# Block products of an MLP's down projection, spread over both up chunks of a pair and summed over the layer

## The chip, the cores and the metric

The kernel runs on 1 core of one Trainium2 chip. The metric is device microseconds of one execution. Before the change it is 2117.61 us, the median of 3 runs (2116.02 to 2118.4). The profile shows one further execution, which took 2115.5 us; its span in the trace is 2113.7 us.

## The reference, cut to what matters

```python
D_MODEL = 2048; SEQ = 256; DEPTH = 2; D_FF = 4 * D_MODEL      # float32

def _mlp(h, w_up, w_down):
    return jnp.square(jax.nn.relu(h @ w_up)) @ w_down

for layer in range(DEPTH):
    ...                                        # attention and pooling (even), gated convolution (odd)
    x = x + _mlp(_rmsnorm(x, mlp_norm_g[layer]), w_mlp_up[layer], w_mlp_down[layer])
```

The change is in `_mlp`, which runs once in each of the two layers: 256 tokens, an up matrix of 2048 x 8192 and a down matrix of 8192 x 2048, 64 MB each. The weights are read from HBM once.

## The kernel before, in words

**Numbers.** TensorE works on float32r, a shortened float32. Every weight and every activation is therefore split into `hi` (its rounded value) and `lo` (the rest). A weight slab of 1 MB (512 rows by 512 columns, tile `raw`, two buffers) arrives by a DMA of SyncE's queue. ScalarE casts half a slab to `hi` (L140), VectorE subtracts to get `lo` (L141), and a ring of six `hi` and six `lo` buffers holds what TensorE is to read next. Three products (hi·hi, hi·lo, lo·hi) make one full product.

**The MLP in chunks.** The 8192 hidden columns are 16 up chunks of 512, taken as 8 pairs. `up_chunk(c)` multiplies the normalised, turned input `xT` with 4 slabs (64 couples of a 128x512 matmul, L160, and a 128x256 matmul, L161), then makes the hidden tile `hT` in two halves: a copy on ScalarE (`t`, L194), a sum on VectorE (`h`, L196), ReLU and square on ScalarE (L728, L730), and a split into hi and lo (L200, L201). The next user of the chunk needs `hT`.

**The down projection.** For the first seven pairs, columns 0 to 1023 of the output are made by `down_seven`: a 2x2 block scheme with seven products instead of eight, on sums and differences of blocks of the weights (`b`, three buffers, 128x2048 each) and of the activations (`fT`, four forms made by `sum_forms` on VectorE and ScalarE). Each product is 12 matmuls (L764 to L766). I call them p1, p5, the one of `form(3)`, p6 (`form(2)`), p7 (`form(0)`), and the two last ones, which read `hT` alone. Columns 1024 to 2047 are made by `down_block(pair, 2)` and `down_block(pair, 3)`, plain blocks of 48 matmuls each (L153 to L155). The eighth pair is made of four plain blocks.

**Sums into x.** The result of a product or a plain block goes from PSUM into the residual `x` with the token's scale `r2`: one VectorE instruction of 128x512 each (`onto`, L790; L850 for the plain blocks). Within a pair, `down_seven` keeps products in SBUF tiles `part` (copied by ScalarE, L779), combines them with 4 additions (L783) and does 7 `onto`: 11 VectorE instructions of 128x512 a pair.

**The order.** Each engine runs its own instructions in a fixed order. The kernel's code is written as generators, and a scheduler orders the instructions of each engine from the order of the calls. Per pair the calls before were: five products, with one slab of the first up chunk (2p+2; I call it chunk A) behind each of the first four; the rest of chunk A; the two last products; the whole second up chunk (2p+3, chunk B); two plain blocks. PSUM has 4 buffers of two banks: chunk A or B takes two, and products (two to a buffer) and plain blocks take the others.

## Time and profile before

| what | us |
|---|---|
| the profiled execution, whole | 2115.5 |
| its span in the trace | 2113.7 |
| TensorE matmuls, busy | 2047.5 |
| VectorE, busy | 1535.1 |
| ScalarE, busy | 1126.1 |
| stretch of the first layer's MLP that holds its pairs | about 327 to 1014 |
| stretch of the second layer's MLP | about 1428 to 2114 |

The page of a profile lists the busy time of each engine, then groups of instructions with the mean time of one and the idle time of the engine just before them, with what ended it. Three more views of the same trace are used below: the waits (who waited for whom, total, times, longest), windows (busy time of each engine and the granted TensorE clock in a stretch), and the timeline (instructions one by one, with start, duration, and in brackets the idle time ahead of them). Matmuls overlap in the timeline, so what one costs is the distance between two starts and not its duration. Times within the trace are counted from the start of the span.

### The profile page before, as it was taken

The numbers are of one execution on the slowest core, as the hardware profiler recorded it, in microseconds if no ns is written. First come the engines' busy times: TensorE is split into PE (matmuls) and PEld (weight loads), VectorE is DVE, ScalarE is ACT, GpSimd is POOL, SyncE is SP. The second block draws the span as 40 slices with busy tenths as digits, with TensorE's granted clock in tenths as the row PEclk, the third lists the DMA queues.
The fourth block names the chain that finished last, engine by engine and source line by source line (L and its number), as shares of the span: only waits on it lengthen the run. The fifth ranks groups of instructions, "written<-read, shape, count | busy, mean of one in ns | idle before, by whom it ended". The sixth has DMA issues, their size and how long they took to land.

```text
span 2113.7 us, 26545 instructions
## 1 busy us (share of the span) xinstructions
PE 2047.5 (97%) x10534; PEld 1745.7 (83%) x10534; DVE 1535.1 (73%) x1843; ACT 1126.1 (53%) x1500; POOL 52.5 (2%) x76
## 2 busy tenths in 40 slices
PE   8999999999999999999999999999999999999999
PEld 8987888778787887888788888887878787787887
DVE  5667659787787877776566656569778787887864
ACT  5466556555555545555444444456555555555552
POOL 1340000000000000000000000000000000000000
PEclk9999999999999999999999999999999999999999
DMA  7554466555656555545555555465565655556544
GB/s 241 167 180 147 142 200 196 179 179 166 211 164 203 173 179 179 173 151 194 199 183 193 182 186 193 159 220 169 190 199 161 212 179 182 176 167 202 168 165 161
DMA packets 195820, 384.20 MB, mean 182 GB/s; under 512 B 6224, under 2 KB 16336, under 8 KB 195696
## 3 DMA queue, kind: packets, MB, share of 16 engines
q1 hardware_dynamic: 195312, 382.23, 55.7%
q8 instruction: 82, 1.34, 0.3%
q0 software_dynamic: 352, 0.27, 0.1%
q14 instruction: 42, 0.34, 0.0%
q10 hardware_dynamic: 32, 0.01, 0.0%
HBM read 380.39 MB, written 2.10 MB: 181 GB/s over the span
## 4 chain that ended last, share of the span: by engine, by line
PE 88%; DVE 6%; ACT 3%; issue 1%; POOL 1%; DMA 1%; SPq 0%; ACTq 0%; DVEq 0%; POOLq 0%
PE ps L160 31%; PE ps L161 16%; PE ps L153 10%; PE ps L155 10%; PE ps L154 10%; PE ps L764 3%; PE ps L766 3%; PE ps L765 3%; DVE lo L141 1%; DVE x L790 1%; DVE part L783 1%; ACT hi L140 1%; DVE hT L201 1%; ACT sq L730 1%; ACT h L728 1%
## 5 line engine op out<-in xcount | busy, mean ns | idle before, releaser
L160 PE MATMUL ps<-xT,hi 128*128 128x512 f32 x2816 | 1016.6, 402 | 3.8 <-ACT hi L140 3.2
L141 DVE TENSOR_TENSOR lo<-raw,hi 128x1024 fp32r<-128x1024 f32 (+2 forms) x610 | 735.9, 1225 | 334.6 <-ACT hi L140 333.1
L140 ACT CAST hi<-raw 128x1024 fp32r<-128x1024 f32 (+2 forms) x610 | 629.3, 1048 | 506.6 <-PE ps L160 141.8
L161 PE MATMUL ps<-xT,lo 128*128 128x256 f32 x2816 | 802.6, 286 | 43.7 <-DVE lo L141 43.5
L160 PEld LDWEIGHTS ps<-xT,hi 128*128 128x128 f32 x2816 | 540.7, 192 | 134.6 <-PE ps L766 5.4
L161 PEld LDWEIGHTS ps<-xT,lo 128*128 128x128 f32 x2816 | 542.0, 192 | 53.7 <-DVE lo L141 49.5
L153 PE MATMUL ps<-hi,hT 128*128 128x512 f32 (+1 forms) x896 | 349.2, 390 | 0.0
L155 PE MATMUL ps<-hi,hT 128*128 128x512 f32 (+1 forms) x896 | 347.5, 388 | 0.0
L154 PE MATMUL ps<-lo,hT 128*128 128x512 f32 (+1 forms) x896 | 347.0, 387 | 0.0
L140 ACT CAST hi<-b 128x1024 fp32r<-128x1024 f32 x196 | 206.0, 1053 | 219.1 <-PE ps L160 118.8
L141 DVE TENSOR_TENSOR lo<-b,hi 128x1024 fp32r<-128x1024 f32 x196 | 238.5, 1220 | 76.2 <-ACT hi L140 76.1
L153 PEld LDWEIGHTS ps<-hi,hT 128*128 128x128 f32 x896 | 168.3, 188 | 35.1 <-issue 1.3
L155 PEld LDWEIGHTS ps<-hi,hT 128*128 128x128 f32 x896 | 168.2, 188 | 34.9
L154 PEld LDWEIGHTS ps<-lo,hT 128*128 128x128 f32 x896 | 168.3, 188 | 33.4
L194 ACT COPY t<-ps 128x512 f32<-128x512 f32 x88 | 50.8, 580 | 70.9 <-PE ps L161 70.9
L764 PE MATMUL ps<-hi,fT 128*128 128x512 f32 x224 | 88.4, 394 | 0.0
L766 PE MATMUL ps<-hi,fT 128*128 128x512 f32 x224 | 87.7, 392 | 0.0
L765 PE MATMUL ps<-lo,fT 128*128 128x512 f32 x224 | 87.1, 389 | 0.0
L196 DVE TENSOR_TENSOR h<-ps,t 128x512 f32<-128x512 f32 x64 | 43.7, 686 | 34.1 <-ACT t L194 34.1
L764 PE MATMUL ps<-hi,hT 128*128 128x512 f32 x168 | 65.8, 393 | 0.2 <-ACT hT L200 0.2
L786 DVE TENSOR_TENSOR b<-b,b 128x2048 f32<-128x2048 f32 x28 | 64.0, 2287 | 2.7 <-DMA b<-in_w_mlp_down 2.2
L765 PE MATMUL ps<-lo,hT 128*128 128x512 f32 x168 | 65.5, 390 | 0.0
(184 smaller groups left out, 1635.7 us busy)
## 6 DMA issues: line engine op xcount, KB each, us to landing
raw<-in_w_mlp_up SPq DMA_DIRECT2D x128, 1024.0 KB, 5.3
raw<-in_w_mlp_down SPq DMA_DIRECT2D x72, 1024.0 KB, 5.2
b<-in_w_mlp_down SPq DMA_DIRECT2D x56, 1024.0 KB, 6.0
raw<-in_odd_w_in SPq DMA_DIRECT2D x48, 1024.0 KB, 5.2
raw<-in_even_w_out SPq DMA_DIRECT2D x16, 1024.0 KB, 5.2
raw<-in_odd_w_out SPq DMA_DIRECT2D x16, 1024.0 KB, 5.3
raw<-in_even_w_in SPq DMA_DIRECT2D x8, 1024.0 KB, 5.6
raw<-in_even_w_in SPq DMA_DIRECT2D x7, 1088.0 KB, 6.6
```

Source lines behind the costliest of these rows:

```text
L140: a = nc.scalar.copy(h, r)
L141: v = nc.vector.tensor_tensor(out=l, in0=r, in1=h.bitcast(F32), op=ALU.subtract)
L153: nc.tensor.matmul(o, lhsT=a_hi, rhs=hi[:, c0:c0 + n], start=first, stop=False)
L154: nc.tensor.matmul(o, lhsT=a_hi, rhs=lo[:, c0:c0 + n], start=False, stop=False)
L155: nc.tensor.matmul(o, lhsT=a_lo, rhs=hi[:, c0:c0 + n], start=False, stop=last)
L160: nc.tensor.matmul(o, lhsT=hi[:, c0:c0 + P], rhs=act[:, kt, :], start=first, stop=False)
L161: nc.tensor.matmul(o[:, S:2 * S], lhsT=lo[:, c0:c0 + P], rhs=act[:, kt, 0:S], start=False, stop=last)
L194: nc.scalar.copy(t, ps[:, :, S:2 * S])
L764: nc.tensor.matmul(o, lhsT=a_hi, rhs=hi, start=q == 0, stop=False)
L765: nc.tensor.matmul(o, lhsT=a_hi, rhs=lo, start=False, stop=False)
L766: nc.tensor.matmul(o, lhsT=a_lo, rhs=hi, start=False, stop=q == 3)
L786: nc.vector.tensor_tensor(out=out_, in0=a, in1=b, op=ALU.subtract)
```

## The change

It does three things in `mlp`, and one beside it.

1. **Order.** `up_chunk` and `down_block` yield more often, and the loop over the pairs calls them so: five products between the four slabs of chunk A as before; then the first half of plain block 2, the end of chunk A (its `hT`), the second half of plain block 2; then the sixth product, a slab of chunk B, the seventh product, the other slabs of chunk B; the first half of plain block 3, the end of chunk B, the second half of plain block 3. So one plain block now stands behind each up chunk, where both stood behind chunk B.
2. **Sums.** p1, p5, p6 and p7 are no longer combined and scaled in each pair. They are added into four SBUF tiles `totals` over the layer (`summed`: ScalarE copies in the first pair, VectorE additions from PSUM in the next six). At the seventh pair four `onto` and four additions bring them into `x`. A pair does 3 `onto` as before for the other three products. The count over a layer falls from 77 to 53 VectorE instructions of 128x512, and from 14 to 4 ScalarE copies.
3. **`hT` by halves.** `up_chunk` yields after each half, so that the scheduler sees the halves apart.
4. **Tiles.** Two small tiles move to pools that are freed earlier, and `R` gets one buffer, which makes room for `totals`. No instruction changes there.

```diff
+            hid[c] = hT
+            if seven:
+                sums[c] = fT
             for i, ps in enumerate(pss):
                 u = sum_halves(ps, "h")
...
                     sum_forms(fT[:, i], sq.rearrange("p e (t s) -> p (e t) s", t=T))
-            hid[c] = hT
-            if seven:
-                sums[c] = fT
+                yield
...
-            def kept(o):
-                part = pools["forms"].tile([P, NB], F32, tag="part", name=uid("part"), bufs=3)
-                nc.scalar.copy(part, o)
-                return part
+            def summed(name, o):
+                if pair == 0:
+                    totals[name] = pools["forms"].tile([P, NB], F32, tag=name, name=uid(name), bufs=1)
+                    nc.scalar.copy(totals[name], o)
+                else:
+                    plus(totals[name], totals[name], o)
...
-            s1 = kept(one[:, 0, :])
+            summed("p1", one[:, 0, :])
...
-            s5 = kept(one[:, 1, :])
-            onto(0, 0, s1)
+            summed("p5", one[:, 1, :])
...
-            plus(s1, two[:, 1, :], s1)
+            summed("p6", two[:, 1, :])
...
-            e = pools["forms"].tile([P, NB], F32, tag="part", name=uid("part"), bufs=3)
-            plus(e, three[:, 0, :], s1)
-            onto(1, 0, e)
-            plus(s1, s1, s5)
-            onto(0, 1, s1)
-            plus(s5, e, s5)
-            onto(1, 1, s5)
+            summed("p7", three[:, 0, :])
...
+            if pair == pairs - 2:
+                onto(0, 0, totals["p1"])
+                plus(totals["p6"], totals["p6"], totals["p1"])
+                plus(totals["p7"], totals["p7"], totals["p6"])
+                onto(1, 0, totals["p7"])
+                plus(totals["p6"], totals["p6"], totals["p5"])
+                onto(0, 1, totals["p6"])
+                plus(totals["p7"], totals["p7"], totals["p5"])
+                onto(1, 1, totals["p7"])
...
                     if i == 0:
                         flush()
+                        yield
...
         for p in range(pairs - 1):
-            products, slabs = down_seven(p), up_chunk(2 * p + 2)
+            products = down_seven(p)
+            slabs, block = up_chunk(2 * p + 2), down_block(p, 2, False)
             next(products)
-            for at in range(5):
+            for at in range(4):
                 next(products)
-                if at < 4:
-                    next(slabs)
-            whole(slabs)
-            whole(products)
-            whole(up_chunk(2 * p + 3))
-            for b in (2, 3):
-                down_block(p, b, False)
+                next(slabs)
+            next(products)
+            for steps in (block, slabs, slabs, block, slabs):
+                next(steps, None)
+            slabs, block = up_chunk(2 * p + 3), down_block(p, 3, False)
+            for steps in (products, slabs, products, slabs, slabs, slabs, block, slabs, slabs, block, slabs):
+                next(steps, None)
```

**Place 1, the end of chunk A (second pair of the first layer).** On TensorE before, the two last products follow p7, and chunk B follows them; these are the last rows of the seventh product (`ps_4209`) and the first of chunk B (`ps_4231`, `ps_4232`):

```order
L764 MATMUL ps_4209<-hi_4214,hT_3683 128x512
L765 MATMUL ps_4209<-lo_4215,hT_3683 128x512
L766 MATMUL ps_4209<-hi_4214,hT_3683 128x512
L160 MATMUL ps_4231<-xT_2333,hi_4235 128x512
L160 MATMUL ps_4232<-xT_2333,hi_4235 128x512
L161 MATMUL ps_4231<-xT_2333,lo_4236 128x256
```

From the end of chunk A to that first `L160` stand 36 matmuls: p7 and the two last products, 12 each. With the change, on TensorE too, p7 (`ps_4117`) is followed by the plain block (`ps_4139`):

```order
L765 MATMUL ps_4117<-hi_4122,fT_3785 128x512
L766 MATMUL ps_4117<-lo_4123,fT_3785 128x512
L767 MATMUL ps_4117<-hi_4122,fT_3785 128x512
L153 MATMUL ps_4139<-hi_4142,hT_3465 128x512
L154 MATMUL ps_4139<-lo_4143,hT_3465 128x512
L155 MATMUL ps_4139<-hi_4142,hT_3465 128x512
```

Behind its 48 matmuls come the 12 of the sixth product and then chunk B, whose first slab has the halves 4269 (lo 4270) and 4273: 72 matmuls instead of 36 stand between the two chunks. The seventh product has moved behind the first slab of chunk B.

On VectorE at the same place before, the sums of the products stand between the steps that make `hT` and `fT`; `lo_4236`, which chunk B waits for, comes four rows behind the last row shown here:

```order
L783 TENSOR_TENSOR part_4146<-ps_4125,part_3880 128x512
L745 TENSOR_TENSOR f_4164<-sq_4160,f_4164 128x128
L790 SCALAR_TENSOR_TENSOR x<-part_4146,r_2931,x 128x512
L783 TENSOR_TENSOR part_3880<-part_3880,part_3949 128x512
L201 TENSOR_TENSOR hT_4153<-sq_4160,hT_4153 128x2x256
L790 SCALAR_TENSOR_TENSOR x<-part_3880,r_2931,x 128x512
L783 TENSOR_TENSOR part_3949<-part_4146,part_3949 128x512
L746 TENSOR_TENSOR f_4164<-sq_4160,f_4164 128x128
L790 SCALAR_TENSOR_TENSOR x<-part_3949,r_2931,x 128x512
L196 TENSOR_TENSOR h_4172<-ps_3883,t_4170 128x512
L201 TENSOR_TENSOR fT_4154<-f_4164,fT_4154 128x512
L790 SCALAR_TENSOR_TENSOR x<-ps_4125,r_2931,x 128x512
```

With the change one addition, that of p7, is left there (`p_3428`; the first half's `h_4178`, a `lo` and an `f` stand ahead of these rows, and the last row is chunk B's first half slab):

```order
L787 TENSOR_TENSOR p_3428<-p_3428,ps_4117 128x512
L746 TENSOR_TENSOR f_4185<-sq_4181,f_4185 128x128
L196 TENSOR_TENSOR h_4193<-ps_3877,t_4191 128x512
L201 TENSOR_TENSOR hT_4174<-sq_4181,hT_4174 128x2x256
L747 TENSOR_TENSOR f_4185<-sq_4181,f_4185 128x128
L141 TENSOR_TENSOR lo_4245<-b_4242,hi_4244 128x1024
L201 TENSOR_TENSOR fT_4175<-f_4185,fT_4175 128x512
L745 TENSOR_TENSOR f_4200<-sq_4196 128x256
L141 TENSOR_TENSOR lo_4249<-b_4242,hi_4248 128x1024
L201 TENSOR_TENSOR hT_4174<-sq_4196,hT_4174 128x2x256
L746 TENSOR_TENSOR f_4200<-sq_4196,f_4200 128x128
L141 TENSOR_TENSOR lo_4270<-raw_4267,hi_4269 128x1024
```

What moved: of the eight sums that stood among these steps (three additions, five `onto`, one of them the row behind those shown) one addition is left at the place, and the two `lo` of the sixth product are new in it.

**Place 2, the end of chunk B.** With the change, one plain block (48 matmuls) stands on TensorE between the end of chunk B and p1 of the next pair, whose last three matmuls read the second half of chunk B's `hT`; before, both plain blocks stood there. These are VectorE's rows from chunk B's `h_4497` to the second half of its `hT_4493`, with the change:

```order
L196 TENSOR_TENSOR h_4497<-ps_4265,t_4495 128x512
L141 TENSOR_TENSOR lo_4569<-b_4561,hi_4568 128x1024
L790 TENSOR_TENSOR b_4561<-b_4629,b_4561 128x2048
L201 TENSOR_TENSOR hT_4493<-sq_4500,hT_4493 128x2x256
L745 TENSOR_TENSOR f_4504<-sq_4500 128x256
L196 TENSOR_TENSOR h_4512<-ps_4266,t_4510 128x512
L746 TENSOR_TENSOR f_4504<-sq_4500,f_4504 128x128
L141 TENSOR_TENSOR lo_4590<-raw_4587,hi_4589 128x1024
L747 TENSOR_TENSOR f_4504<-sq_4500,f_4504 128x128
L141 TENSOR_TENSOR lo_4594<-raw_4587,hi_4593 128x1024
L201 TENSOR_TENSOR fT_4494<-f_4504,fT_4494 128x512
L201 TENSOR_TENSOR hT_4493<-sq_4515,hT_4493 128x2x256
```

The subtraction of two weight blocks (`b_4561`, 128x2048) for the next pair's p5 now stands ahead of `hT`; before it stood behind both halves.

**Place 3, SyncE's queue at the end of chunk A.** With the change the slabs of the plain block (`raw_4140`, `raw_4206`) stand among blocks `b`, whose transfers wait until VectorE has read the buffer that they reuse:

```order
L128 DMA raw_4075<-in_w_mlp_up 128x4x512
L128 DMA raw_4140<-in_w_mlp_down 128x4x512
L758 DMA b_4242<-in_w_mlp_down 128x4x512
L128 DMA raw_4206<-in_w_mlp_down 128x4x512
L758 DMA b_4561<-in_w_mlp_down 128x4x512
L128 DMA raw_4267<-in_w_mlp_up 128x4x512
```

Before, the sixth product's block stood at the same place and chunk B's slabs behind it. What moved is that a slab of a plain block now waits behind `b_4242`, and chunk B's first slab behind `b_4561`, a block of the next pair.

## The prediction

> **What bounds the kernel now.** I read the page first, then the waits of TensorE, then windows and timelines around one wait.

> ```profile
> span 2113.7 us, 26545 instructions
> PE 2047.5 (97%) x10534; PEld 1745.7 (83%) x10534; DVE 1535.1 (73%) x1843; ACT 1126.1 (53%) x1500; POOL 52.5 (2%) x76
> L161 PE MATMUL ps<-xT,lo 128*128 128x256 f32 x2816 | 802.6, 286 | 43.7 <-DVE lo L141 43.5
> ```

> TensorE is busy 97% of the span and VectorE 73%, so the sum of VectorE's work binds nothing; it can only be late somewhere. The third row says where: the second matmul of a chunk's couple, which needs `lo`. The waits of TensorE over the whole span, and then those between 940 and 1050 us alone, give the number of times:

> ```profile
> PE ps L161 <- DVE lo L141: 43.5, 13, 3.6
> ...
> PE ps L160 <- ACT hi L140: 3.2, 1, 3.2
> PE ps L161 <- DVE lo L141: 0.2, 1, 0.2
> ```

> One of the 13 is 0.2 us, at the end of the first layer's MLP; the other 12 share 43.3 us, 3.6 each. Going through the span stretch by stretch I find one at the end of chunk A in pairs one to six of each layer, and none in the seventh, whose chunks need no forms. Here is one, on TensorE's timeline (p7 begins at 545.37; the fourth row holds two couples' first matmuls):

> ```profile
> 545.37 0.39 PE L764 MATMUL ps<-hi,fT 128*128 128x512 f32 x1
> ...
> 553.36 0.39 PE L766 MATMUL ps<-hi,hT 128*128 128x512 f32 x1
> 553.59 0.91 PE L160 MATMUL ps<-xT,hi 128*128 128x512 f32 x2
> 558.12 0.58 PE L161 MATMUL ps<-xT,lo 128*128 128x256 f32 x1 [3.62 <-DVE lo L141]
> ...
> 560.63 0.63 PE L160 MATMUL ps<-xT,hi 128*128 128x512 f32 x1
> ...
> 564.33 0.40 PE L160 MATMUL ps<-xT,hi 128*128 128x512 f32 x1
> ...
> 564.68 0.40 PE L160 MATMUL ps<-xT,hi 128*128 128x512 f32 x1
> ```

> 36 matmuls fill 545.37 to 553.59, so one product matmul takes 8.22 / 36 = 0.228 us; a couple takes 564.68 - 564.33 = 0.35 us. After the wait the matmuls are slower for a while. The windows say why (columns: busy time and instructions of the engines, then the granted clock):

> ```profile
> 553.50:558.10 4.60, 0.95 (x4) 0.24 (x2) 4.52 (x8) 2.15 (x4) 0.00 (x0) 0.83 0.00 0
> 558.10:563.30 5.20, 5.18 (x17) 4.51 (x18) 4.37 (x6) 0.62 (x1) 0.00 (x0) 0.50 0.53 158
> 563.30:582.00 18.70, 18.70 (x108) 16.29 (x107) 9.44 (x8) 8.01 (x8) 0.00 (x0) 1.00 0.73 237
> ```

> The clock is 0.50 for about 5.2 us behind the wait, and 1.00 afterwards. So a wait costs itself and some 2 us more. VectorE is busy 4.52 of the 4.60 us in which TensorE waits: it is the one that is late. Its timeline from the end of chunk A on:

> ```profile
> 545.49 0.69 DVE L196 TENSOR_TENSOR h<-ps,t 128x512 f32<-128x512 f32 x1 [0.53 <-ACT t L194]
> ...
> 548.41 0.68 DVE L783 TENSOR_TENSOR part<-ps,part 128x512 f32<-128x512 f32 x1
> 549.01 0.28 DVE L745 TENSOR_TENSOR f<-sq,f 128x128 f32<-128x128 f32 x1
> 549.21 0.74 DVE L790 SCALAR_TENSOR_TENSOR x<-part,r,x 128x512 f32<-128x512 f32 x1
> 549.88 0.68 DVE L783 TENSOR_TENSOR part<-part,part 128x512 f32<-128x512 f32 x1
> ...
> 553.21 0.68 DVE L196 TENSOR_TENSOR h<-ps,t 128x512 f32<-128x512 f32 x1
> 553.81 0.69 DVE L201 TENSOR_TENSOR fT<-f,fT 128x512 fp32r<-128x512 f32 x1
> 554.42 1.41 DVE L790 SCALAR_TENSOR_TENSOR x<-ps,r,x 128x512 f32<-128x512 f32 x2
> ...
> 556.51 0.42 DVE L744 TENSOR_TENSOR f<-sq 128x256 f32<-128x256 f32 x1
> 556.84 1.22 DVE L141 TENSOR_TENSOR lo<-raw,hi 128x1024 fp32r<-128x1024 f32 x1
> 557.98 0.28 DVE L745 TENSOR_TENSOR f<-sq,f 128x128 f32<-128x128 f32 x1
> ```

> Chunk B's `lo` ends near 558.06, 12.6 us after `h` began, and TensorE had 8.2 us of products to bridge it plus 0.5 us for two hi matmuls. That leaves 4.05 us from 554.06 to 558.12. Distances of starts give the prices: an addition or a step of `hT` 0.60 (553.21 to 553.81), an `onto` 0.67, a `lo` 1.14, an `f` 0.34 or 0.20.

> **What one wait costs** has a control in the trace: chunk B with the wait (sixth pair) and without it (seventh), from its first matmul to the first of the plain block behind it, in four rows of the timeline:

> ```profile
> 830.44 0.91 PE L160 MATMUL ps<-xT,hi 128*128 128x512 f32 x2
> ...
> 859.39 0.39 PE L153 MATMUL ps<-hi,hT 128*128 128x512 f32 x1
> ...
> 922.83 0.40 PE L160 MATMUL ps<-xT,hi 128*128 128x512 f32 x1
> ...
> 945.65 0.39 PE L153 MATMUL ps<-hi,hT 128*128 128x512 f32 x1
> ```

> 28.95 against 22.82 us for the same matmuls: 6.13 us a wait. The bound from the other side is the wait taken apart: 4.05 us idle, and 5.2 us at half clock that do 2.6 us of work, 6.65 in all. I take 6.13, which is measured whole.

> **The change part by part.**

> *Order at the end of chunk A.* The matmuls between chunk A and chunk B go from 36 to 72: 72 x 0.228 = 16.4 us of cover. VectorE's rows there, from `h` to chunk B's first `lo`: 4 `lo` (4.56), 6 steps at 0.60 (two `h`, two `hT`, one `fT`, the p7 addition; 3.60), two `f` at 0.34 and three at 0.20 (1.28), 9.4 us. With about 1 us in which `h` and `sq` come from ScalarE, as the gaps before 548.41 show, chunk B's `lo` is ready 10.4 us after chunk A. 6 us are left, and the 12 waits go: 12 x 6.13 = 73.6 us.

> *Sums.* 24 VectorE instructions and 10 ScalarE copies fewer a layer, some 15 us of VectorE's busy time a layer. TensorE hides all VectorE work that isn't late, so beyond the wait they count nothing; they do make the 9.4 us above, in place of what would be 7 sums more, 4.6 us. With the sums left in, the 10.4 would be 15 and the cover would still just hold: most of the gain comes from the order. A sum that reads PSUM costs what one from SBUF does (548.41 and 549.88, both 0.68). The 8 instructions at the seventh pair (5 us) stand in chunk B, where VectorE needs about 1.14 us for each half slab and TensorE 8 couples, 2.8 us. Cost 0; uncovered they would cost 5 us a layer.

> *PSUM.* The plain block takes the buffer that the `form(3)` product and p6 had. Its first matmul must wait for the p6 addition, which follows p6 by two `lo` (some 2 us) while 16 couples and p7 (5.6 + 2.7 us) lie between: 0.

> *Order at the end of chunk B.* This is the tightest place. The cover falls from two plain blocks to one: 48 matmuls and the first 9 of p1, 57 x 0.228 = 13.0 us, until the second half of `hT` is read. VectorE's rows until then: 3 `lo` (3.42), 5 steps (3.00), an `f` of 0.34 and two of 0.20, and the subtraction of blocks, whose group row is

> ```profile
> L786 DVE TENSOR_TENSOR b<-b,b 128x2048 f32<-128x2048 f32 x28 | 64.0, 2287 | 2.7 <-DMA b<-in_w_mlp_down 2.2
> ```

> 2.29 us, in sum 9.5. With 1 us of waits for ScalarE it is 10.5, so 2.5 us are left. Cost 0 as long as nothing more than that is added; from there on what is added costs itself, 12 times.

> *SyncE.* The plain block's second slab stands behind `b_4242`, whose buffer is free when b22 + b11 is done, ahead of p6. The rows of the page's DMA issues:

> ```profile
> raw<-in_w_mlp_down SPq DMA_DIRECT2D x72, 1024.0 KB, 5.2
> b<-in_w_mlp_down SPq DMA_DIRECT2D x56, 1024.0 KB, 6.0
> ```

> Its own buffer is free once chunk A's last slab is split, which the ring of six `hi` and `lo` allows from about 11 us before the chunk's end. It lands 5.2 us later, some 5 us before that end, and is needed 2.7 + 5.5 us after it. Cost 0. The other edits (two tiles, `R`) move no instruction: 0.

> **The sum** is made against the profiled execution: 2115.5 - 73.6 = 2041.9, with 6.65 a wait 2035.7. That execution lies 2.1 us below the median of the runs shown, so a median may come out that much higher, 2044. I give 2042.

> [...]

> **The rivals.**

> 1. *A small wait at the end of chunk B.* For it: 2.5 us of margin under a ScalarE queue that I have only bounded by gaps elsewhere. Against: in the trace before, the same chain took 590.13 + 0.68 - 582.82 = 8.0 us at this place, without the 2.29 us:

> ```profile
> 582.82 0.69 DVE L196 TENSOR_TENSOR h<-ps,t 128x512 f32<-128x512 f32 x1 [1.67 <-ACT t L194]
> ...
> 590.13 0.68 DVE L201 TENSOR_TENSOR hT<-sq,hT 128x512 fp32r<-128x512 f32 x1
> ```

> [...]
> 2. *The change doesn't take the wait away.* If the late `lo` were due to something that moves with it (a slab, ScalarE), the time stays near 2115. Against: VectorE has no gap between 548.41 and 557.98.
> 3. *Slower: SyncE's queue.* If `raw_4206` behind `b_4242` arrives so late that TensorE idles 4 us in the plain block, one such wait in all 14 pairs costs 14 x 6.13 = 85.8 us, more than the 73.6 gained: 2128. It decides from 5.3 us of net loss a pair, so from a slab that comes some 15 us later than worked out above. In the stretch before the wait no row of TensorE's waits names a DMA, which speaks against it.

> **How the numbers follow.** Forecast, no wait left: 2042, between 2034 and 2048, chance 0.78. Small wait without half clock (2054 to 2066) 0.08, with it (2085) 0.04. No effect, or most of the wait left (2100 to 2116) 0.05. Slower (2128) 0.04. Below 2034 0.01. The range 2034 to 2062 holds the forecast, and the small wait's lower part, 0.80 in all with what I may have missed. About 0.2% is what a measurement of this kernel can tell from no change, 4 us: faster 0.93, within 0.03, slower 0.04.

> **What would show it.** In the profile of the changed kernel: no wait of TensorE for `lo` L141 of over 1 us within the pairs; a granted clock of 1.00 in every stretch of the pairs; a chunk A end every 86 us instead of 92 (545.45 - 453.23 in two rows of the chain that ended last); TensorE at 98 to 99% of its span; VectorE busy about 30 us less. Step by step: chunk B's first `lo` 6 us ahead of its matmul, and p1 right behind the plain block. Chunk A's ends, second and third pair, before:

> ```profile
> 453.23 1.05 ACT hi L140
> ...
> 545.45 1.05 ACT hi L140
> ```

> Wrong would be a wait at L765 on `hT`, a wait at L154 on a slab, or a clock below 1.00 without a wait.

## The result, and the profile after

The changed kernel takes 2038.84 us, the median of 4 runs (2038.12 to 2039.72), beside 2118.01 us for the kernel before on the same chip: a ratio of 0.9627, with a 95% interval of 0.9611 to 0.9644. It is faster by 3.7%, some 79 us. The profiled execution took 2038.12 us. Its page begins so (span, then busy time, share and instructions of each engine), and its chain of what ended last follows:

```profile
span 2036.3 us, 26507 instructions
...
PE 2013.3 (99%) x10534; PEld 1726.1 (85%) x10534; DVE 1503.7 (74%) x1795; ACT 1115.8 (55%) x1480; POOL 52.5 (3%) x76
...
PE 97%; DMA 1%; ACT 1%; DVE 1%; issue 0%; SPq 0%; POOL 0%; DVEq 0%; ACTq 0%
...
L161 PE MATMUL ps<-xT,lo 128*128 128x256 f32 x2816 | 791.1, 281 | 0.2
```

The group of L161 had 43.7 us of idle time ahead of it, 43.5 of it due to `lo`. Now it has 0.2. VectorE lost 48 instructions and 31.4 us of busy time. The span is 77.4 us shorter. Three stretches show where that went, first before and then after: the first layer's MLP, the odd layer, the second layer's MLP (windows: start and end, length, busy time and instructions of each engine, granted clock, then DMA).

```profile
283.00:1014.00 731.00, 708.67 (x3523) 597.93 (x3522) 568.14 (x632) 404.95 (x496) 0.20 (x2) 0.97 0.56 181
1017.00:1382.00 365.00, 364.63 (x1956) 313.25 (x1956) 218.94 (x258) 162.54 (x190) 0.95 (x7) 1.00 0.56 186
1383.00:2113.70 730.70, 705.28 (x3529) 595.72 (x3529) 565.31 (x623) 396.41 (x474) 0.00 (x0) 0.98 0.57 184
```

```profile
282.00:973.00 691.00, 690.84 (x3524) 587.69 (x3522) 552.53 (x609) 399.90 (x486) 0.21 (x2) 1.00 0.61 195
976.00:1342.00 366.00, 365.83 (x1956) 314.58 (x1956) 218.48 (x258) 162.34 (x190) 0.94 (x7) 0.99 0.55 181
1343.00:2036.00 693.00, 689.33 (x3529) 587.24 (x3529) 550.14 (x600) 391.90 (x464) 0.00 (x0) 1.00 0.60 194
```

The last window of the changed kernel stops 0.3 us before its span ends, so the two MLPs are 40.0 and 37.4 us shorter, and the rest moved by about 1 us. In the first layer's MLP TensorE is now idle for 0.16 us out of 691. The end of chunk A in the second pair, VectorE's timeline:

```profile
446.08 0.69 DVE L196 TENSOR_TENSOR h<-ps,t 128x512 f32<-128x512 f32 x1 [0.53 <-ACT t L194]
...
449.01 0.68 DVE L787 TENSOR_TENSOR p<-p,ps 128x512 f32<-128x512 f32 x1
...
455.23 1.21 DVE L141 TENSOR_TENSOR lo<-raw,hi 128x1024 fp32r<-128x1024 f32 x1
...
531.71 0.69 DVE L196 TENSOR_TENSOR h<-ps,t 128x512 f32<-128x512 f32 x1 [0.53 <-ACT t L194]
```

and TensorE's, in the same pair (p7, the plain block, the product of `hT` alone, chunk B):

```profile
445.96 0.39 PE L765 MATMUL ps<-hi,fT 128*128 128x512 f32 x1
...
448.71 0.39 PE L153 MATMUL ps<-hi,hT 128*128 128x512 f32 x1
...
459.59 0.39 PE L765 MATMUL ps<-hi,hT 128*128 128x512 f32 x1
...
462.31 0.40 PE L160 MATMUL ps<-xT,hi 128*128 128x512 f32 x1
```

Between chunk A and chunk B lie 462.31 - 445.96 = 16.35 us. Chunk B's first `lo` ends near 456.4, 10.4 us after chunk A and 6 us ahead of its matmul. A pair lasts 531.71 - 446.08 = 85.63 us; the same distance in the trace before was 92.2.

### The profile page after: what moved, and what is told of

Read it like the earlier page. It is cut to its first block, busy times and chain, and to the rows that moved or that the text cites. A ratio compares the mean times of both kernels' runs of the same rounds, so it can differ in the third digit from the quotient of the medians.

```text
span 2036.3 us, 26507 instructions
## 1 busy us (share of the span) xinstructions
PE 2013.3 (99%) x10534; PEld 1726.1 (85%) x10534; DVE 1503.7 (74%) x1795; ACT 1115.8 (55%) x1480; POOL 52.5 (3%) x76
## 4 chain that ended last, share of the span: by engine, by line
PE 97%; DMA 1%; ACT 1%; DVE 1%; issue 0%; SPq 0%; POOL 0%; DVEq 0%; ACTq 0%
PE ps L160 32%; PE ps L161 16%; PE ps L153 10%; PE ps L155 10%; PE ps L154 10%; PE ps L765 4%; PE ps L767 4%; PE ps L766 4%; PE ps L166 1%; PE ps L168 1%; PE ps L167 1%; DMA raw<-in_even_w_in 1%; PE ps L297 1%; ACT hi L140 0%; DVE lo L141 0%; PE ps L614 0%
## 5 line engine op out<-in xcount | busy, mean ns | idle before, releaser
L160 PE MATMUL ps<-xT,hi 128*128 128x512 f32 x2816 | 993.3, 395 | 3.3 <-ACT hi L140 3.3
L141 DVE TENSOR_TENSOR lo<-raw,hi 128x1024 fp32r<-128x1024 f32 (+2 forms) x610 | 739.3, 1226 | 331.5 <-ACT hi L140 327.9
L140 ACT CAST hi<-raw 128x1024 fp32r<-128x1024 f32 (+2 forms) x610 | 633.2, 1049 | 508.4 <-PE ps L160 206.5
L161 PE MATMUL ps<-xT,lo 128*128 128x256 f32 x2816 | 791.1, 281 | 0.2
L160 PEld LDWEIGHTS ps<-xT,hi 128*128 128x128 f32 x2816 | 530.5, 188 | 126.6 <-ACT hi L140 3.7
L161 PEld LDWEIGHTS ps<-xT,lo 128*128 128x128 f32 x2816 | 529.2, 188 | 5.3 <-DVE lo L141 1.4
L153 PE MATMUL ps<-hi,hT 128*128 128x512 f32 (+1 forms) x896 | 349.1, 390 | 0.0
L154 PE MATMUL ps<-lo,hT 128*128 128x512 f32 (+1 forms) x896 | 347.2, 387 | 0.0
L140 ACT CAST hi<-b 128x1024 fp32r<-128x1024 f32 x196 | 204.5, 1051 | 207.8 <-PE ps L160 161.6
L141 DVE TENSOR_TENSOR lo<-b,hi 128x1024 fp32r<-128x1024 f32 x196 | 237.6, 1220 | 44.9 <-ACT hi L140 44.6
L153 PEld LDWEIGHTS ps<-hi,hT 128*128 128x128 f32 x896 | 168.3, 188 | 35.0 <-issue 1.3
L154 PEld LDWEIGHTS ps<-lo,hT 128*128 128x128 f32 x896 | 168.3, 188 | 33.6 <-DVE lo L141 0.4
L765 PE MATMUL ps<-hi,fT 128*128 128x512 f32 x224 | 88.1, 393 | 0.0
L766 PE MATMUL ps<-lo,fT 128*128 128x512 f32 x224 | 87.1, 389 | 0.0
L194 ACT COPY t<-ps 128x512 f32<-128x512 f32 x88 | 50.8, 578 | 53.6 <-PE ps L161 53.6
L858 DVE SCALAR_TENSOR_TENSOR x<-ps,r,x 128x512 f32<-128x512 f32 (+1 forms) x73 | 52.0, 739 | 19.3 <-PE ps L155 19.3
L765 PE MATMUL ps<-hi,hT 128*128 128x512 f32 x168 | 65.8, 392 | 0.2 <-ACT hT L200 0.2
L767 PE MATMUL ps<-hi,hT 128*128 128x512 f32 x168 | 65.6, 391 | 0.0
L766 PE MATMUL ps<-lo,hT 128*128 128x512 f32 x168 | 65.3, 389 | 0.0
## 6 DMA issues: line engine op xcount, KB each, us to landing
raw<-in_w_mlp_up SPq DMA_DIRECT2D x128, 1024.0 KB, 5.4
raw<-in_w_mlp_down SPq DMA_DIRECT2D x72, 1024.0 KB, 5.1
b<-in_w_mlp_down SPq DMA_DIRECT2D x56, 1024.0 KB, 6.0
raw<-in_odd_w_in SPq DMA_DIRECT2D x48, 1024.0 KB, 5.2
raw<-in_even_w_out SPq DMA_DIRECT2D x16, 1024.0 KB, 5.2
raw<-in_odd_w_out SPq DMA_DIRECT2D x16, 1024.0 KB, 5.3
raw<-in_even_w_in SPq DMA_DIRECT2D x8, 1024.0 KB, 5.7
```

The lines of the kernel that those rows point to most:

```text
L140: a = nc.scalar.copy(h, r)
L141: v = nc.vector.tensor_tensor(out=l, in0=r, in1=h.bitcast(F32), op=ALU.subtract)
L153: nc.tensor.matmul(o, lhsT=a_hi, rhs=hi[:, c0:c0 + n], start=first, stop=False)
L154: nc.tensor.matmul(o, lhsT=a_hi, rhs=lo[:, c0:c0 + n], start=False, stop=False)
L160: nc.tensor.matmul(o, lhsT=hi[:, c0:c0 + P], rhs=act[:, kt, :], start=first, stop=False)
L161: nc.tensor.matmul(o[:, S:2 * S], lhsT=lo[:, c0:c0 + P], rhs=act[:, kt, 0:S], start=False, stop=last)
```

## The experiments

The question was what of this the order brings and what the sums, whether VectorE's lateness at one place is the whole cause, and how much room the new order has. Beside the runs of the order alone, the sums alone and of 18 and 24 extra instructions the kernel before took 2114.72 us, beside the next four 2116.68; with the ratio above the changed kernel would stand at 2035.8 and 2037.7 there. What a pair costs more is worked out against these, over 12 pairs.

### The order alone

The new order of calls, with the sums of before put back into every pair:

```diff
-            summed("p1", one[:, 0, :])
+            s1 = kept(one[:, 0, :])
...
-            summed("p7", three[:, 0, :])
+            e = pools["forms"].tile([P, NB], F32, tag="part", name=uid("part"), bufs=3)
+            plus(e, three[:, 0, :], s1)
+            onto(1, 0, e)
...
+            onto(1, 1, s5)
```

> The new call order (72 matmuls between chunk A and chunk B), with the products' sums as before: a ScalarE copy or a VectorE addition per product and the combinations onto x in every pair. My theory: the gain is the 12 waits for chunk B's lo, and the order alone covers them. VectorE has up to 7 sums (4.6 us) more between chunk A's end and that lo, 15 us against 16.4 us of cover, so no wait of over 1 us on lo within the pairs and a chunk A end every 85.6 to 87 us: 2037 to 2045 us, TensorE busy 98 to 99%, VectorE busy some 30 us more than with the change whole. Rival (the sums are what counts; the order only moves the wait): waits on lo or on a block's lo come back at chunk A's end, 1 to 4 us each, 2055 to 2118 us.

Measured: 2036.07 us, ratio 0.9633 (0.9617 to 0.9648). Its page has VectorE back at its old number of instructions:

```profile
PE 2012.8 (99%) x10534; PEld 1726.6 (85%) x10534; DVE 1527.5 (75%) x1843; ACT 1127.5 (55%) x1500; POOL 52.7 (3%) x76
```

No wait for `lo` L141 stands among TensorE's waits. The order alone brings the whole gain; 24 us of VectorE's busy time more cost nothing.

### The sums alone

The calls in the order of before, with the four running totals of the change:

```diff
-            s1 = kept(one[:, 0, :])
+            summed("p1", one[:, 0, :])
...
+            if pair == pairs - 2:
+                onto(0, 0, totals["p1"])
...
+                onto(1, 1, totals["p7"])
```

> The call order of before (36 matmuls between chunk A and chunk B), with the four running sums combined in the seventh pair only. VectorE's rows from h to chunk B's first lo are then 5.4 us in sum, some 6.5 us with the gaps for ScalarE, against 8.7 us of cover; the second half's lo is ready some 11.3 us after chunk A's end and wanted 11.2 us after it. If the 12 waits are nothing but VectorE being 4.05 us late, 4.6 us less on VectorE take them away as well: at most 0.5 us a wait is left, clock 1.00, 2037 to 2048 us; the two halves of the change are then each enough and their gains don't add up. Rival (my prediction's wording that most of the gain comes from the order, read as: the sums alone bring little): waits of 1 to 3 us stay, 2065 to 2110 us.

Measured: 2040.6 us, ratio 0.9649 (0.9633 to 0.9665). The sums alone bring the whole gain as well, to within some 0.2% of the time, which is what the intervals can tell. VectorE at the end of chunk A, and TensorE's first couple of chunk B:

```profile
449.28 0.69 DVE L196 TENSOR_TENSOR h<-ps,t 128x512 f32<-128x512 f32 x1 [0.53 <-ACT t L194]
...
454.40 1.22 DVE L141 TENSOR_TENSOR lo<-raw,hi 128x1024 fp32r<-128x1024 f32 x1
```

```profile
457.38 0.40 PE L160 MATMUL ps<-xT,hi 128*128 128x512 f32 x1
457.62 0.28 PE L161 MATMUL ps<-xT,lo 128*128 128x256 f32 x1
```

The `lo` is ready at 455.5, 2 us early, where it was some 4 us late before. So the two halves of the change are not two gains that add up: each takes away the same 12 waits.

### Neither: five instructions written later

If it is VectorE's queue at that place alone, then nothing has to be saved or moved on TensorE. This is the kernel before; only the last five instructions of the combination behind p7 are written behind chunk B's first slab:

```diff
             plus(e, three[:, 0, :], s1)
-            onto(1, 0, e)
...
-            onto(1, 1, s5)
+            def rest():
+                onto(1, 0, e)
...
+                onto(1, 1, s5)
+            later.append(rest)
...
-            whole(up_chunk(2 * p + 3))
+            slabs = up_chunk(2 * p + 3)
+            next(slabs)
+            later.pop()()
+            whole(slabs)
```

> The kernel of before, its call order and all its sums; only the last five instructions of the combination behind p7 (three onto, two additions) are written behind chunk B's first slab, so VectorE splits that slab first. No instruction more or less on any engine, TensorE's order the same. Theory (VectorE is late at that one place by what its queue holds ahead of the lo): the first lo is ready some 6.2 us after chunk A's end against 8.6 us of cover, the next three 0.1 to 0.5 us before they are wanted: waits of at most 0.5 us, 2035 to 2048 us, with VectorE as busy as before. Rival (it is VectorE's amount of work or the PSUM and SBUF traffic around it, not its order): the waits move to the next lo or stay, 2070 to 2118 us.

Measured: 2040.86 us, ratio 0.9639 (0.9622 to 0.9656). VectorE's page row and its timeline at the place:

```profile
PE 2016.9 (99%) x10534; PEld 1726.9 (85%) x10534; DVE 1530.7 (75%) x1843; ACT 1121.0 (55%) x1500; POOL 53.0 (3%) x76
```

```profile
447.88 0.69 DVE L196 TENSOR_TENSOR h<-ps,t 128x512 f32<-128x512 f32 x1 [0.53 <-ACT t L194]
...
453.00 1.22 DVE L141 TENSOR_TENSOR lo<-raw,hi 128x1024 fp32r<-128x1024 f32 x1
...
459.13 0.74 DVE L790 SCALAR_TENSOR_TENSOR x<-part,r,x 128x512 f32<-128x512 f32 x1
459.79 0.68 DVE L783 TENSOR_TENSOR part<-part,part 128x512 f32<-128x512 f32 x1
```

The same 1843 instructions on VectorE, the same call order, no instruction fewer on any engine. TensorE's order is that of before too, but for the couples of chunk B's first slab, which are paired a little differently. The `lo` comes 5.1 us after `h` where it came 11.4 us after it (545.49 to 556.84 in the trace before), and the instructions at 459.13 and 459.79, which stood ahead of it, now stand behind. This settles the cause: it was what VectorE's queue held ahead of one `lo`. The time stands 3 us above the 2037.7 of the changed kernel, which the intervals of the two ratios don't tell apart.

### How much room the end of chunk A has

Extra VectorE instructions, with no use, in the changed kernel at the end of chunk A in pairs one to six; 18, 21 and 24 of them:

```diff
+                if i == 1 and c % 2 == 0 and 2 <= c < 2 * pairs - 2:
+                    for j in range(18):
+                        nc.vector.tensor_tensor(out=u[:, j % 2, :], in0=sq[:, j % 2, :], in1=sq[:, j % 2, :], op=ALU.max)
                 split(hT[:, 2 * i:2 * i + 2, 0:S], hT[:, 2 * i:2 * i + 2, S:2 * S], sq)
```

> The changed kernel with 18 more VectorE instructions of 128x256 (each u = max(sq, sq) into a dead tile, some 0.34 us) at the end of chunk A in pairs one to six, before the second half of hT: 6.1 us. By the trace of the change the own product's second lo of the block is then ready 463.1 against 461.2 in that pair, so a wait of 1.9 us in 12 places (on a block's lo or chunk B's lo). [...] Rival (every wait of that size brings half clock too): 12 x 4, 2085 to 2095 us with a clock of 0.50 for some us. Rival (the margin of 6 us was not there, or is larger): over 2110 or under 2045.

Measured: 2061.09 us, +2.1 us a pair, clock 0.997 over the span, as in the changed kernel. That is near the 1.9 us of the wait alone, and not the 4 us a pair of the first rival. TensorE's waits, and the place itself:

```profile
PE ps L769 <- DVE lo L141: 7.7, 10, 0.8
PE ps L161 <- DVE lo L141: 6.2, 13, 1.3
```

```profile
463.68 0.62 PE L160 MATMUL ps<-xT,hi 128*128 128x512 f32 x2
464.18 0.47 PE L768 MATMUL ps<-hi,hT 128*128 128x512 f32 x1
465.42 0.50 PE L769 MATMUL ps<-lo,hT 128*128 128x512 f32 x1 [0.77 <-DVE lo L141]
```

It is the block's `lo` (L769) that comes late first, and not chunk B's. The trace records 0.77 us there, counted from the recorded end of the matmul at 464.18, but from start to start it is 465.42 - 464.18 - 0.23 = 1.01 us, where 0.23 is what a product matmul costs without a wait: this wait cost 0.24 us more than its record. With as much for each of the two waits of a pair, the 1.2 us recorded (7.7 + 6.2 us and 0.9 for `hi`, over 12) make 1.7 of the 2.1 us; the rest is not accounted for. The first row shows something else: the scheduler has drawn the first matmuls of two couples of chunk B ahead of the product's last matmuls. It sets TensorE's order when the kernel is built, so the extra instructions have changed that order as well.

> The same with 24 such instructions, 8.2 us: the wait becomes some 3.7 to 4.2 us, about what the 12 waits of before were, but in the middle of a block's product and not inside a run of couples. Theory (idle plus some 5 us at half clock, 6.1 to 6.7 us a wait): 12 x 6.4 = 77 us, 2105 to 2125 us, and a clock of 0.50 behind each wait. Rival (the wait alone): 12 x 4 = 48, 2085 to 2090. On the pace of couples: if it is the wait itself that slows chunk B's couples from 0.349 to 0.353 us, they are slow here too; if it needs the wait to fall inside a run of couples, they stay at 0.349.

Measured: 2099.54 us, 5.3 us a pair, below the range. The idle time recorded is 2.9 us a pair and not 3.7 to 4.2, because those couples fill some of it. The half clock came in 10 of the 12 places (windows of 1 us through the span), for 3.4 or 6.8 us. Most of the idle time, 23.6 of 34.9 us, is no longer put down to a `lo` but to the plain block's sum into `x` (L861), which stands ahead of that `lo` in VectorE's queue; what TensorE needs from it is not shown:

```profile
469.03 0.47 PE L768 MATMUL ps<-hi,hT 128*128 128x512 f32 x1 [2.16 <-DVE x L861]
470.27 0.80 PE L769 MATMUL ps<-lo,hT 128*128 128x512 f32 x1 [0.77 <-DVE lo L141]
```

```profile
466.70:469.60 2.90, 0.65 (x2) 0.19 (x1) 2.90 (x7) 1.06 (x2) 0.00 (x0) 0.98 0.00 0
469.60:476.10 6.50, 5.83 (x17) 4.87 (x18) 5.64 (x7) 1.18 (x2) 0.00 (x0) 0.50 0.61 173
```

> Between the runs with 18 and 24 extra instructions at the end of chunk A: VectorE 1.0 us less late than with 24, so some 1.9 to 2.1 us of idle time in a pair in place of 2.9. At 18 (1.1 us idle) the clock stayed at 1.00, at 24 (2.2 and 0.8 us with one matmul between) it fell to 0.50. If the clock falls on what is idle within some 3.4 us, it stays at 1.00 here: 12 x 3.0 above the changed kernel, 2068 to 2078 us. Rival (it falls from some 2 us of idle time on): 2090 to 2100 us.

Measured: 2074.19 us, 3.0 us a pair for 2.0 us of recorded idle time, inside the first range, but the clock did not stay at 1.00 throughout: it fell in 2 of the 12 places (intervals of 3.413 us as in the last section). One of them:

```profile
467.50:470.70 3.20, 3.20 (x11) 2.45 (x10) 2.85 (x3) 1.05 (x1) 0.00 (x0) 0.50 0.70 196
```

So the price of VectorE's lateness here is nothing for some 4 us (6.0 us late less the 2.1 that they cost; no run with fewer than 18 shows the edge itself), then about itself, and where the half clock falls, that on top (0.50 in 2 of 12 places at 2.0 us of recorded idle time, in 10 of 12 at 2.9). What the traces show of when it falls is in the last section.

### How much room the end of chunk B has

The same instructions at the place that the prediction called the tightest, ahead of the first half of chunk B's `hT` (`i == 0 and c % 2 == 1`), 6 and 12 of them:

> The changed kernel with 6 extra VectorE instructions of 128x256 (2.0 us) at the end of chunk B in pairs one to six, ahead of the first half of hT. By my prediction 2.5 us (2.8 in the trace) are to spare there until p1 wants hT's second half: no wait on hT. But in the order that the scheduler makes of it, the lo of p5's block now stands behind two onto and the sum of p1: it would be ready at 503.9 against 501.25 wanted. Theory by that order: a wait of up to 2.7 us on that lo, 12 times, 2058 to 2070 us. Rival (the margin of 2.5 us holds for all that is wanted there): 2035 to 2042 us.

Measured: 2037.01 us, ratio 0.9625. The rival was right: 2.0 us more on VectorE cost nothing. My theory, read off the order of VectorE's instructions alone, fell.

> The same with 12 such instructions, 4.0 us: hT's second half some 2 us late for p1 (wait at p1), then p5's lo 2.8 us late. Theory: both waits, 4.7 us in 12 places; without half clock 2092 us, with it 2115 to 2125 us. Rival (one margin of 2.5 to 2.8 us, and what exceeds it costs itself): 12 x 1.4 = 17, 2050 to 2056 us.

Measured: 2042.3 us, ratio 0.9650 (0.9631 to 0.9669), against 2037.7: 0.4 us a pair for 4.0 us of VectorE's time, less than either theory and no more than the intervals of the two ratios leave open. In the place of the 24 waits that the theory asked for, TensorE's waits hold one of 0.6 us on `hT` and one of 0.5 on `lo` in the whole span, and neither lies in the twelve places (1395.51 and 979.79 us). VectorE and TensorE at the end of chunk B, second pair:

```profile
502.86 0.68 DVE L201 TENSOR_TENSOR hT<-sq,hT 128x512 fp32r<-128x512 f32 x1
```

```profile
501.38 0.39 PE L770 MATMUL ps<-hi,hT 128*128 128x512 f32 x1
501.60 0.40 PE L160 MATMUL ps<-xT,hi 128*128 128x512 f32 x1
...
502.32 0.50 PE L768 MATMUL ps<-hi,hT 128*128 128x512 f32 x1
502.65 0.39 PE L769 MATMUL ps<-lo,hT 128*128 128x512 f32 x1
502.88 0.28 PE L161 MATMUL ps<-xT,lo 128*128 128x256 f32 x1
...
503.92 0.39 PE L770 MATMUL ps<-hi,hT 128*128 128x512 f32 x1
```

p1 has 12 matmuls. Nine run, then the scheduler puts couples of the next chunk A (L160, L161) between the last three, the last of which (L770, at 503.92) reads the `hT` of 502.86. The lateness is covered by other work: the next chunk's slab was there and had PSUM to go to. As at the end of chunk A, this is the order that the scheduler made for this kernel, not the order of the changed kernel held still.

### The start of the odd layer

One longer wait is left in the changed kernel, 3.3 us for `hi` between the first layer's MLP and the odd layer, with half clock behind it (0.50 from 975.80 to 982.63). Here two squares on ScalarE are put behind the two `hi`:

```diff
             turn_block(xT, b, which, i)
-            squares(ss, b)
+            if which == "mix1" and b == 3:
+                with behind(*last_prep[:1]):
+                    squares(ss, b)
+            else:
+                squares(ss, b)
```

> The changed kernel; at the start of the odd layer the last two squares for the norm on ScalarE are issued behind the two hi of that layer's first slab, not ahead of them. In the changed kernel TensorE waits 3.25 us there for hi and then runs some 6 us at half clock. ScalarE reached that hi at 975.05 and the last matmul that reads the buffers under it started at 972.49, so hi could come up to 2 us sooner. Theory (a wait of 1.1 to 1.5 us costs itself alone, as in the run with 18 instructions): 2.0 us of the wait and some 3 us of half clock go, 5 us in all, 2029 to 2034 us where the changed kernel gives 2036 in the same call; and if the slower pace of the couples in the odd layer (0.353 against 0.349 us at clock 1.00) is what half clock leaves behind, up to 3 us more. Rival (hi waits for something else, and the squares only fill its wait): no change, within 1 us of the changed kernel.

> The changed kernel itself, beside the run above on the same chip: 2034 to 2040 us.

Measured: 2035.8 us, ratio 0.9611 (0.9597 to 0.9624), beside 2035.59 us, 0.9617 (0.9603 to 0.9630), for the changed kernel. That is no difference beside the spread of 2 to 3 us between the executions of each. `hi` did come sooner (at 971.76, where it was 975.05), and the wait moved on to the `lo` behind it, with half clock until 980:

```profile
976.39 0.39 PE L161 MATMUL ps<-xT,lo 128*128 128x256 f32 x1 [2.17 <-DVE lo L141]
```

Neither theory had this: the cover of one late operand was the lateness of the next. No version here beats the change.

## Why the prediction was right, point by point

**The bound.** Right. The 12 waits on `lo` were the loss, and they are gone; the clock is 1.00 over both MLPs. That VectorE's queue at one place was the cause is shown by the run with five instructions written later.

**The price of a wait.** Right in kind, too small by some 3%. I took 6.13 us and had 6.65 as the other bound. From the first `h` of chunk A's end to the seventh it is 552.7 and 550.9 us in the two layers before, 513.8 in both after: 76.1 us for 12 waits, 6.3 each. It isn't one number. Two pairs of the trace before, by the starts of `h` at chunk A's end:

```profile
361.87 0.69 DVE L196 TENSOR_TENSOR h<-ps,t 128x512 f32<-128x512 f32 x1 [0.48 <-ACT t L194]
...
453.27 0.69 DVE L196 TENSOR_TENSOR h<-ps,t 128x512 f32<-128x512 f32 x1 [0.53 <-ACT t L194]
...
637.90 0.69 DVE L196 TENSOR_TENSOR h<-ps,t 128x512 f32<-128x512 f32 x1 [0.53 <-ACT t L194]
```

The first lasts 91.40 us, the third 637.90 - 545.49 = 92.41, that is 5.8 and 6.8 us over 85.63. The main part of the difference is how long the half clock lasts: 3.4 us in five of the 12 places, whose pairs take 91.5 us in the mean, and 6.8 in the other seven, with 92.3. The last section shows one of each.

My control, the seventh pair's chunk B, was itself a little slow: its couples run at 0.353 us and not the 0.349 of the changed kernel (last section), 64 x 0.004 = 0.26 us that the control hid.

**Small waits and the half clock.** No run shows the terms behind the two times of the small wait (2054 to 2066 and 2085), waits of 1 to 2 us at the end of chunk B: no wait stood in its twelve places even with 4.0 us more on VectorE. What waits of that size cost is shown at the end of chunk A: 1.2 us of recorded idle time a pair cost 2.1 us, with the clock at 0.997 over the span as in the changed kernel; 2.0 us cost 3.0, with half clock in 2 places of 12; 2.9 us (2.16 and 0.77 with one matmul between in the place shown) cost 5.3, with half clock in 10 of 12. Nor did the half clock at 558 come only behind the wait: it began at 556.55, when TensorE had stood for 2.5 us (from 554.06) and was to stand until 558.12. So a wait of 2 us was not safe from half clock here.

**Order at the end of chunk A.** Right: 10.4 us worked out, 10.4 measured, 6 us to spare for chunk B's `lo`. But that was not the margin of the place. With VectorE 6.0 us later, the product of `hT` alone waited first, for the `lo` of its block, and the cost was 2.1 us a pair: by the difference the room is about 4 us. I had looked for the wait that was there before, and not for the next operand of the same queue.

**Sums.** "Most of the gain comes from the order" is the step that failed. I had both numbers, 4.05 us of wait and 4.6 us of sums taken out, and didn't set one against the other. The sums alone suffice, the order alone suffices, and together they bring no more than either, as far as the intervals tell. That the sums cost nothing on the path beyond the wait was right: 24 us of VectorE's time put back made no difference.

**Order at the end of chunk B.** The numbers were right: In the trace after, VectorE's part of `hT` ended 10.1 us after chunk B where 10.5 was worked out, some 3 us before it was wanted. The step "from there on what is added costs itself" was wrong: 4.0 us more cost 0.4 by the medians, which is within the noise, and no wait is recorded at any of the twelve places. The calls alone don't fix TensorE's order; the scheduler, when it builds the kernel, draws the next chunk's couples forward. Rival 1, a small wait at this place, did not come.

**PSUM and SyncE's queue.** Cost 0, as predicted: no wait of TensorE in the pairs names a slab, and the third rival did not come.

**The sum.** 2115.5 - 73.6 = 2041.9 against 2038.12 for the profiled execution and 2038.84 for the median. Of the 3.8 us between 2041.9 and 2038.12, 2.5 are the price of a wait (76.1 - 73.6), and 1.3 lie outside the twelve places.

## What to carry to other kernels

When an engine that isn't the bound makes the bound wait, look at what stands ahead of the late instruction in its queue, before any work is taken out: here five instructions written later gave what a new order or 48 instructions fewer gave. Two remedies for one wait don't add up; set each against the wait's size (here 4.05 us against 8 us more cover, 4.6 us of sums fewer, or a `lo` 6.2 us sooner) to see which is enough alone. A margin holds for one operand: ask what the same queue delivers next, and whether the waiting engine has other work that can be drawn forward. And the price of a wait isn't the wait alone: here 4.05 us cost 6.3, and two short waits close together (2.16 and 0.77 us in the place shown) had half clock behind them in 10 places of 12, as the wait of 4.05 us had in all 12 before.

## What was not expected of the hardware

```profile
372.23:375.64 3.41, 1.09 (x7) 1.01 (x8) 3.34 (x6) 0.07 (x1) 0.00 (x0) 1.00 0.02 5
375.64:379.05 3.41, 3.41 (x12) 2.93 (x12) 3.26 (x5) 0.62 (x1) 0.00 (x0) 0.50 0.60 160
379.05:382.46 3.41, 3.41 (x21) 2.96 (x21) 0.06 (x1) 1.14 (x2) 0.00 (x0) 1.00 1.01 336
...
553.14:556.55 3.41, 1.31 (x5) 0.56 (x3) 3.33 (x7) 2.51 (x5) 0.00 (x0) 1.00 0.00 0
556.55:559.96 3.41, 1.84 (x6) 1.65 (x7) 3.41 (x7) 0.33 (x1) 0.00 (x0) 0.50 0.00 0
559.96:563.37 3.41, 3.41 (x13) 2.92 (x12) 2.51 (x3) 0.29 (x1) 0.00 (x0) 0.50 0.83 249
```

```profile
739.09:742.50 3.41, 1.83 (x9) 1.17 (x7) 3.41 (x9) 1.93 (x2) 0.00 (x0) 1.00 0.00 0
742.50:745.91 3.41, 2.04 (x7) 1.17 (x8) 3.41 (x6) 1.00 (x2) 0.00 (x0) 1.00 0.18 31
```

The first number behind the length is TensorE's busy time. In the twelve traces, from 250 us on, there are 36 intervals at full clock with 1.69 us of it or less, and half clock followed each of them; there are 64 with 1.78 us to 2.9, and it followed none. The trace before has 13 of the 36 (0.20 to 1.69 us) and 4 of the 64 (1.84 to 2.52). So in these traces the two cases part between 1.69 and 1.78 us of 3.41, by the recorded times; that half of the interval is what counts, 1.71 us, is an estimate from these two numbers. In the last two rows the grid cuts the idle time of the place in two, 1.83 and 2.04 us busy, and the clock stayed at 1.00; in ten other places of that run it fell. At 375.64 the half clock came when TensorE had already gone on, and lasted one interval; at 556.55 it came in the middle of the wait, and lasted two.

**Couples have two paces at the same granted clock.** The distance from one L160 to the next is 0.349 us in some stretches and 0.353 in others, with no wait between and the clock at 1.00: in the trace before 0.349 from 284 to 328 us, and 0.353 from 1054 to 1286. The same kernel shows both in the same place: here is the odd layer between 1005 and 1240 us in two executions of the changed kernel, the first from the trace after, the second from its run beside the odd layer's test.

```profile
1005.00:1240.00 235.00, 235.00 (x1331) 204.84 (x1331) 147.68 (x181) 101.08 (x109) 0.62 (x6) 1.00 0.57 185
```

```profile
1005.00:1240.00 235.00, 235.00 (x1349) 205.84 (x1348) 149.55 (x182) 102.17 (x111) 0.62 (x6) 1.00 0.58 188
```

TensorE is busy throughout in both, and does 1331 matmuls in one and 1349 in the other; the spans of these executions differ by 2.7 us (2036.3 and 2033.6). In the pairs of the trace before, the slower pace stands behind the stretch at half clock in 8 of the 12 places (0.353 from 567 on, for one) and not in the other 4 (0.349 from 475 on), and twice, from 927 and from 2026 on, without half clock ahead of it; behind the plain blocks the couples are back at 0.349 (607 us). Its cause stays open. The 18 matmuls fewer are 3.1 us at 235 / 1349 us each: by this estimate the pace alone can make two executions of this kernel differ by some 3 us.
